# Inputs laid out by the host as the products read them, and keys projected turned, in a one-core decoder step

## The chip, the core and the metric

The kernel runs on one core of a Trainium2 chip. The core has TensorE (matrix products and transposes, results in PSUM), VectorE, ScalarE and POOL (GpSimd) for elementwise work, SP (SyncE) as the queue that issues most DMAs, and 16 DMA engines. The engines run their instructions in the order in which they were written down and wait for each other by semaphores. The metric is the device time of one execution in microseconds (us). Arrays that the Python function `kernel()` rearranges before the launch, and results that it rearranges after it, lie outside that time.

## The reference

One step of a decoder layer with 1024 features, for a prompt of 2048 tokens and for 8 sampled sequences of 8 new tokens, all in float32. The parts that matter here:

```python
z = jnp.einsum('bsd,dc->bsc', x, w_in)            # queries, keys, values, gates, mLSTM q/k/v
conv = conv_b + xpad[:, 0:S] * conv_w[0]          # + 3 more taps; then silu: mLSTM q and k
fox_h = _fox_prompt(fq, fk, fv, flogf)            # causal attention, 8 heads of 64, forget terms
(C, n, m), m_h = _mlstm_prompt(mq, mk, mv, ig, lf)
k_past = cache_k[l][page_table].reshape(DB, past, FOX_HEADS, FOX_HEAD_DIM)   # 8 x 8192 keys
sfox_h = _fox_sample(sq, sk, sv, slogf, k_past, v_past, logf_past)
mix = jnp.concatenate([fox_h, mn], axis=-1) @ w_o
x1 = _layer_norm(DN_ALPHA * x + mix, ln1_g, ln1_b)
hid = jnp.square(jax.nn.relu(x1 @ w1))
y = _layer_norm(DN_ALPHA * x1 + hid @ w2, ln2_g, ln2_b)
```

Besides y, new keys and values, log forget values, the mLSTM states and the last three columns of the convolution's input are returned.

## The kernel before

Each large product is made of three (`mm3`, L154 to L156): both operands are split into a high part (`split_hi`, ScalarE, L146) and a rest (`split_lo`, VectorE, L149), and high by high, high by rest and rest by high are summed in PSUM.

The work comes in stages.

*Projections (0 to 962 us).* `block_a` runs over four blocks of 512 tokens; block 0 also has the 64 sampled tokens as tile 16. `x_load` (L281) brings a tile of 128 tokens by 1024 features into one of two buffers named xn. `x_turn` transposes it on TensorE (L296, eight transposes for each tile), because a product contracts over partitions, and splits the result out of PSUM into xh and xl. `wload` (L249) brings 512 rows by 256 columns of w_in and splits them into whi and wlo. Products come in two forms. In `natural`, tokens are the stationary operand and the result has tokens on partitions (values, gates, keys). In the turned form, weights are stationary and the result has features on partitions (mLSTM q and k, queries). All products of this stage, and the transposes px, take PSUM from the same four buffers. `conv_setup` brings the convolution's weights and states and transposes them; at the end of blocks 0 and 3 the new convolution states are transposed back (cs_n L523 to L525, ch_n L531 to L533) for their outputs. Beside the projections run the mLSTM (`m_block`, `m_sample`) and the cached attention.

*Causal attention (to 1415 us), `phase_b`.* Keys are read back from the output k_prompt in groups of 512 tokens by 64 features (dup, L915), doubled by a POOL copy (L916), turned by four TensorE transposes (L936) and split into ks. Queries (L947) were stored turned and are read twice by two DMAs. Then come scores (L974, L975), exponentials (ScalarE, L1000), transposes of the weights (L1013) and products with values (L1022).

*Output projection (to 1656 us), `phase_o`*, with pieces of w_o (`half_wo`), and *feed-forward (to the end), `phase_c`*, in four blocks of tokens with pieces of w1 and w2 (wr, L1121).

*Cached attention, `sample_attention`.* A generator of 294 steps that runs beside the other stages: after so many microseconds of other products by the code's own estimates (`tick`, 5.6 in the projections, 5 from the output projection on) one more step is written down. Cached keys come by indirect DMAs on POOL's queue (`k_gather`, L1521) into a ring of pieces kT; two steps later VectorE transposes them in squares of 32 by 32 (`k_turn`, L1527); two steps after that `qk_step` (L1550) multiplies them with the queries, four heads side by side in the array. Values are gathered by `v_gather` (L1638) and multiplied by `pv_step` (sO, L1662). The keys of the new tokens are transposed on TensorE (L1472) out of a tile sqk.

The order of the instructions on each engine is set at compile time by the framework, which simulates a timeline (`schedule_with_timeline_sim=True`); a few orders are forced by hand (`first` for the first eight loads, `issue_after` for the steps of the generators). An instruction that comes too early on an engine holds up what is behind it.

Of the kernel before, what the change touches and what calls it, by code (L numbers as in the profile page):

```python
# [10 lines left out]
F32 = mybir.dt.float32  # L11
# [41 lines left out]
def body(ctx, tc, I, O, stages):  # L53
# [36 lines left out]
    sqk = []  # L90
# [92 lines left out]
    w_in = I["w_in"][0]  # L183
# [12 lines left out]
    def conv_setup():  # L196
        cwn = pa.tile([5, 1024], F32, name="cwn", tag="xn", bufs=2)
        SY.dma_start(cwn[0:4], I["conv_w"][0])
        SY.dma_start(cwn[4:5], I["conv_b"])
        pcw = ppa.tile([128, 8, 5], F32, name="px", tag="pm", bufs=4)  # L200
# [3 lines left out]
        scn = pa.tile([24, 1024], F32, name="scn", tag="xn", bufs=2)  # L204
        SY.dma_start(scn, I["state_conv"][0].rearrange("b j c -> (b j) c"))
        pcs = ppa.tile([128, 8, 24], F32, name="px", tag="pm", bufs=4)
        for j in range(8):
            T.transpose(pcs[:, j], scn[:, j * 128:(j + 1) * 128], ident[:24, :24])
        V.tensor_copy(scT.rearrange("p j b k -> p j (b k)"), pcs)
# [31 lines left out]
    def wload(cols):  # L241
# [17 lines left out]
    k_out = lambda t: (O["k_sample"].rearrange("l b t h d -> (l b t) (h d)") if t == 16  # L259
                       else O["k_prompt"].rearrange("l b s h d -> (l b s) (h d)")[t * 128:(t + 1) * 128])  # L260
# [17 lines left out]
    def x_load(*tiles):  # L278
        for t in tiles:
            xns[t] = pa.tile([128, D], F32, name="xn", bufs=2)  # L280
            first(SY.dma_start(xns[t][:tok_n(t)], x_of(t)))  # L281

    def x_turn(bi, t):
# [7 lines left out]
        xn = xns.pop(t)  # L291
        (xh, xl), s = xcol(bi, t)
        for hf in range(2):
            px = ppa.tile([128, 4, 128], F32, name="px", tag="pm", bufs=4)
            for k in range(4):
                T.transpose(px[:, k, :n], xn[:n, (hf * 4 + k) * 128:(hf * 4 + k + 1) * 128], ident[:n, :n])  # L296
# [132 lines left out]
    def block_a(bi):  # L429
# [3 lines left out]
        def natural(sink, *cols, hook=None, after=None):  # L433
            wh, wl = W0.pop() if W0 else wload(cols)
# [42 lines left out]
        for j in range(8):  # L477
            if j % 2 == 0:
                wh, wl = wload([(C_QK + j * 128, 256)])
# [37 lines left out]
        if pre:  # L517

            cs_n = pa.tile([24, 1024], F32, name="cs_n", tag="xn", bufs=2)
            for hf in range(2):  # L520
                pc = ppa.tile([24, 512], F32, name="px", tag="pm", bufs=4)
                for j in range(4):
                    T.transpose(pc[:, j * 128:(j + 1) * 128], scT[:, hf * 4 + j].rearrange("p b k -> p (b k)"), ident)  # L523
                A.copy(cs_n[:, hf * 512:(hf + 1) * 512], pc)
            SY.dma_start(O["conv_sample"].rearrange("l b j c -> (l b j) c"), cs_n)  # L525
        if bi == 3:
            ch_n = pa.tile([3, 1024], F32, name="ch_n", tag="xn", bufs=2)
            for hf in range(2):
                pc = ppa.tile([3, 512], F32, name="px", tag="pm", bufs=4)
                for j in range(4):  # L530
                    T.transpose(pc[:, j * 128:(j + 1) * 128], hist[:, hf * 4 + j], ident)  # L531
# [1249 lines left out]
```

## Time and profile before

| what | value |
|---|---|
| three runs | 3441.78, 3434.79, 3453.91 us; median 3441.78 |
| profiled execution, span from first to last instruction | 3435.1 us |
| TensorE busy | 3305.7 us (96%) |
| VectorE, ScalarE, POOL busy | 2174.9, 1365.7, 886.5 us |
| DMA | 646.37 MB, mean 188 GB/s |

The profile gives no other time for the profiled execution than its span. "PE" is TensorE's products and transposes, "PEld" its weight loads, "DVE" VectorE, "ACT" ScalarE. A row for a group names its line, engine and operation, the tiles written and read ("out<-in"), its shape and count, then its busy time and the mean of one instruction, then the idle time of its engine ahead of it and what ended that. A row of waits reads: who waited for whom, us in total, times, longest. TensorE's instructions overlap, so the mean duration of one is longer than the distance from one start to the next, and it is this distance that a product costs. "PEclk" is the clock granted to TensorE as a share of full speed.

### The profile page before, as it was taken

Reading aid. Unit: us, or ns where it says so; the run is one execution under the profiler, and the core shown is the slowest. Engines: PE = TensorE matmul, PEld = TensorE weight load, DVE = VectorE, ACT = ScalarE, POOL = GpSimd, SP = SyncE. Lnnn points to the kernel's source line nnn. Section 1 sums busy time; section 2 is a strip of 40 time slices with the busy share of each in tenths; the row PEclk is TensorE's granted clock in tenths of the full one; section 3 lists DMA queues with packets and bytes.
Section 4 is the critical chain, followed back from the end, with each engine's and each line's share of the span. In section 5 each row is a group of like instructions: output and inputs, shape, how many; then the busy total and the mean of one; then the engine's idle time right before and its main releaser. Section 6 shows DMA issues by size and latency. Waiting matters only on the chain.

```text
span 3435.1 us, 59551 instructions
## 1 busy us (share of the span) xinstructions
PE 3305.7 (96%) x22428; PEld 2682.1 (78%) x22428; DVE 2174.9 (63%) x5286; ACT 1365.7 (40%) x2818; POOL 886.5 (26%) x957
## 2 busy tenths in 40 slices
PE   9999998999989999999999999999999999999998
PEld 8998988888866666677777777777777777888887
DVE  5857757557468887655666667656666545645545
ACT  3333333233358888512323233332333333433332
POOL 0021221322322222276333324323234210100000
PEclk9999999999989999999999999999999999999999
DMA  6565765866653232487877768757669554432221
GB/s 177 141 193 161 238 203 164 271 221 205 224 173 92 74 80 60 154 290 250 292 254 230 260 195 314 267 192 272 230 217 313 197 183 145 164 122 85 82 80 65
DMA packets 428119, 646.37 MB, mean 188 GB/s; under 512 B 84092, under 2 KB 320960, under 8 KB 426936
## 3 DMA queue, kind: packets, MB, share of 16 engines
q1 hardware_dynamic: 351144, 363.35, 35.2%
q0 software_dynamic: 74304, 270.57, 21.5%
q10 hardware_dynamic: 2384, 8.65, 0.7%
q8 instruction: 177, 2.90, 0.3%
q14 instruction: 110, 0.90, 0.1%
HBM read 589.63 MB, written 52.83 MB: 187 GB/s over the span
## 4 chain that ended last, share of the span: by engine, by line
PE 75%; DMA 9%; DVE 6%; issue 5%; ACT 2%; POOL 2%; another core or an unknown queue 0%; SPq 0%; POOLq 0%; ACTq 0%; DVEq 0%
PE py L154 7%; PE py L156 7%; PE py L155 7%; PE ph L156 6%; PE ph L155 6%; PE ph L154 6%; PE po L1022 4%; PE pt L1013 4%; PE pm L154 4%; PE pm L156 4%; PE pm L155 4%; PE sO L1662 3%; PE sQ L1550 3%; DMA kT<-cache_k,idxK 2%; PE pS L974 2%
## 5 line engine op out<-in xcount | busy, mean ns | idle before, releaser
L1345 DVE TENSOR_TENSOR y<-y,py 128x512 f32<-128x512 f32 (+1 forms) x476 | 321.0, 681 | 335.1 <-PE py L156 307.3
L154 PE MATMUL ph<-x1h,wh 128*128 128x512 f32 (+1 forms) x1280 | 455.2, 356 | 3.8 <-ACT wh L146 1.8
L156 PE MATMUL ph<-x1h,wl 128*128 128x512 f32 (+1 forms) x1280 | 452.4, 355 | 3.3 <-DVE wl L149 2.4
L155 PE MATMUL ph<-x1l,wh 128*128 128x512 f32 (+1 forms) x1280 | 453.9, 355 | 1.1 <-DVE x1l L149 0.9
L154 PE MATMUL py<-wh,hh 128*128 128x512 f32 (+1 forms) x1088 | 436.1, 403 | 10.2 <-DVE y L1345 6.9
L1521 POOL DMA_INDIRECT kT<-cache_k,idxK x256 | 263.1, 1028 | 702.2 <-PE sQ L1550 641.6
L146 ACT ACTIVATE wh<-wr 128x1024 fp32r<-128x1024 f32 x268 | 277.5, 1055 | 416.0 <-PE py L156 189.8
L1527 DVE STREAM_TRANSPOSE kT<-kT 128x512 f32<-128x512 f32 x512 | 330.0, 685 | 177.5 <-DMA kT<-cache_k,idxK 161.2
L156 PE MATMUL py<-wh,hl 128*128 128x512 f32 (+1 forms) x1088 | 430.5, 396 | 0.0
L155 PE MATMUL py<-wl,hh 128*128 128x512 f32 (+1 forms) x1088 | 430.5, 396 | 0.0
L149 DVE TENSOR_TENSOR wl<-wr,wh 128x1024 fp32r<-128x1024 f32 x268 | 336.2, 1259 | 70.0 <-ACT wh L146 21.0
L154 PE MATMUL pm<-whi,xh 128*128 128x256 f32 (+2 forms) x1088 | 321.6, 296 | 13.5 <-ACT ch_n L532 4.1
L155 PE MATMUL pm<-wlo,xh 128*128 128x256 f32 (+2 forms) x1088 | 315.6, 290 | 1.2 <-DVE wlo L149 0.8
L156 PE MATMUL pm<-whi,xl 128*128 128x256 f32 (+3 forms) x1088 | 315.0, 290 | 1.2 <-issue 1.2
L154 PEld LDWEIGHTS ph<-x1h,wh 128*128 128x128 f32 x1280 | 241.2, 188 | 45.0 <-issue 6.5
L156 PEld LDWEIGHTS ph<-x1h,wl 128*128 128x128 f32 x1280 | 241.4, 189 | 39.5 <-DVE wl L149 4.6
L155 PEld LDWEIGHTS ph<-x1l,wh 128*128 128x128 f32 x1280 | 241.2, 188 | 37.8 <-issue 2.9
L154 PEld LDWEIGHTS py<-wh,hh 128*128 128x128 f32 (+1 forms) x1088 | 201.2, 185 | 73.0 <-issue 14.1
L156 PEld LDWEIGHTS py<-wh,hl 128*128 128x128 f32 (+1 forms) x1088 | 201.3, 185 | 53.2 <-issue 2.5
L155 PEld LDWEIGHTS py<-wl,hh 128*128 128x128 f32 (+1 forms) x1088 | 201.7, 185 | 44.1 <-issue 2.5
L154 PE MATMUL pm<-xh,whi 128*128 128x256 f32 (+1 forms) x768 | 225.7, 294 | 6.0 <-ACT qi L495 6.0
L1638 POOL DMA_INDIRECT vt<-cache_v,idxV x158 | 165.2, 1046 | 242.7 <-PE sO L1662 162.8
(369 smaller groups left out, 6892.4 us busy)
## 6 DMA issues: line engine op xcount, KB each, us to landing
wr<-w SPq DMA_DIRECT2D x256, 512.0 KB
wra<-w_in SPq DMA_DIRECT2D x112, 512.0 KB
Rb<-dR SPq DMA_DIRECT2D x128, 128.0 KB
xn<-x_prompt SPq DMA_DIRECT2D x16, 512.0 KB
qn<-dq SPq DMA_DIRECT2D x128, 64.0 KB
wr<-w_o SPq DMA_DIRECT2D x16, 512.0 KB
xr<-dmix SPq DMA_DIRECT2D x16, 512.0 KB
y<-x_prompt SPq DMA_DIRECT2D x16, 512.0 KB
```

The costliest lines, as they stand in the source:

```text
L146: last["ACT"] = A.activation(dst, src, AF.Copy, scale=scale)
L149: r = (eng or V).tensor_tensor(dst, src, hi.bitcast(F32), op=OP.subtract)
L154: T.matmul(ps, wh, xh, start=first, stop=False)
L155: T.matmul(ps, wh, xl, start=False, stop=False)
L156: last["PE"] = T.matmul(ps, wl, xh, start=False, stop=stop)
L1013: T.transpose(pt[:, k], sc[i][0][k0 // 4][:, k * 128:(k + 1) * 128], ident)
L1022: last["PE"] = T.matmul(po[c:c + 64, q0:], z["vn"][:, k], PT[:, k - k0, q0:], start=(k < 2), stop=(k >= nk - 2), skip_group_check=True)
L1345: V.tensor_tensor(y, y, ps, op=OP.add)
L1521: G.indirect_dma_start(out=piece(n), out_offset=None, in_=ck, in_offset=IO(ap=idxK[:, b, j // 2, j % 2:j % 2 + 1], axis=0))
L1527: V.transpose(x, x)
L1550: r = T.matmul(pq[h4 * 32:h4 * 32 + 32, hg].rearrange("p (k f c) -> p k f c", k=2, f=4), z["qb"][:, hd], kv, start=(db == 0), stop=(db == ...
L1638: G.indirect_dma_start(out=vt.rearrange("p f c -> p (f c)"), out_offset=None, in_=cv, in_offset=IO(ap=idxV[:, b, (kt % 4) * 4 + kt // 4, f ...
```

## The change

`kernel()` lays out, before the launch, x (each tile turned, features on partitions), the cached keys (per page, in two halves of four heads each, 32 features by 1024 values of head, feature half and token), the convolution's weights and states, the mLSTM normaliser, and all pieces of w_in, w1 and, for the output projection of the prompt, w_o as contiguous [128, n] arrays. It also turns six results back after the launch. On the chip the transposes for these go (px, pcw, pcs, cs_n, ch_n, nn, pn_), and `k_turn` with its VectorE transposes. Keys are projected in the turned form by the loop of the queries, stored as k_prompt [512, 2048], and read back by two DMAs for each group of 512 tokens, as queries are; the POOL copy and the transposes L936 go, and so does the tile sqk with its transposes.

```diff
-        cwn = pa.tile([5, 1024], F32, name="cwn", tag="xn", bufs=2)
...
-        for j in range(8):
-            T.transpose(pcw[:, j], cwn[:, j * 128:(j + 1) * 128], ident[:5, :5])
-        V.tensor_scalar(cw, pcw, 0.5, None, op0=OP.mult)
...
+        SY.dma_start(cw, I["conv_wb"])
+        V.tensor_scalar(cw, cw, 0.5, None, op0=OP.mult)
+        SY.dma_start(scT, I["state_conv"])
...
-    def wload(cols):
+    def wload(*cols):
...
-            wr = pa.tile([128, 4 * 272], F32, name="wra", bufs=2)[:, :4 * n].rearrange("p (k c) -> p k c", k=4)
-            o = 0
-            for c0, m in cols:
-                first(SY.dma_start(wr[:, :, o:o + m], w_in[kg * 512:(kg + 1) * 512, c0:c0 + m].rearrange("(k p) c -> p k c", p=128)))
-                o += m
+            wr = pa.tile([128, 4 * 272], F32, name="wra", bufs=2)[:, :4 * n]
+            first(SY.dma_start(wr, dap(I["w_in"], w_at[cols] + kg * 512 * n, [[4 * n, 128], [1, 4 * n]])))
+            wr = wr.rearrange("p (k c) -> p k c", k=4)
...
-            first(SY.dma_start(xns[t][:tok_n(t)], x_of(t)))
+            n = 8 * tok_n(t)
+            first(SY.dma_start(xns[t][:, :n], I["xs_t"] if t == 16 else I["xp_t"][t]))
...
-        xn = xns.pop(t)
+        xn = xns.pop(t)[:, :8 * n].rearrange("p (k c) -> p k c", k=8)
         (xh, xl), s = xcol(bi, t)
-        for hf in range(2):
-            px = ppa.tile([128, 4, 128], F32, name="px", tag="pm", bufs=4)
-            for k in range(4):
-                T.transpose(px[:, k, :n], xn[:n, (hf * 4 + k) * 128:(hf * 4 + k + 1) * 128], ident[:n, :n])
-            dh = xh[:, hf * 4:hf * 4 + 4, s]
-            split_hi(dh, px[:, :, :n])
-            split_lo(xl[:, hf * 4:hf * 4 + 4, s], px[:, :, :n], dh)
+        split_hi(xh[:, :, s], xn)
+        split_lo(xl[:, :, s], xn, xh[:, :, s])
...
-            cs_n = pa.tile([24, 1024], F32, name="cs_n", tag="xn", bufs=2)
-            for hf in range(2):
-                pc = ppa.tile([24, 512], F32, name="px", tag="pm", bufs=4)
-                for j in range(4):
-                    T.transpose(pc[:, j * 128:(j + 1) * 128], scT[:, hf * 4 + j].rearrange("p b k -> p (b k)"), ident)
-                A.copy(cs_n[:, hf * 512:(hf + 1) * 512], pc)
-            SY.dma_start(O["conv_sample"].rearrange("l b j c -> (l b j) c"), cs_n)
+            SY.dma_start(O["conv_sample"], scT)
...
-            ch_n = pa.tile([3, 1024], F32, name="ch_n", tag="xn", bufs=2)
...
-            SY.dma_start(O["conv_prompt"].rearrange("l b j c -> (l b j) c"), ch_n)
+            SY.dma_start(O["conv_prompt"], hist)
...
-        for j in range(4):
+        for j in range(8):
+            c, jj = divmod(j, 4)
             if j % 2 == 0:
-                wh, wl = wload([(j * 128, 256)])
+                wh, wl = wload((j * 128, 256))
                 if pre:
                     qr = ps_.tile([32, 8, 8, 8], F32, name="qr", tag="vt", bufs=2)
             cs = slice((j % 2) * 128, (j % 2) * 128 + 128)
+            scale = 1.0 if c else 0.125
...
+                    if c:
+                        st = pa.tile([128, 256], F32, name="st", bufs=4)[:, :64]
+                        A.copy(st, ps[:, 0:64])
+                        SY.dma_start(O["k_sample"][jj * 128:(jj + 1) * 128], st)
...
-                A.activation(st, ps[:, w - 256:], AF.Copy, scale=0.125)
-                SY.dma_start(dq[j, :, t0 + i * 256:t0 + i * 256 + 256], st)
+                A.activation(st, ps[:, w - 256:], AF.Copy, scale=scale)
+                a = t0 + i * 256
+                SY.dma_start(O["k_prompt"][jj * 128:(jj + 1) * 128, a:a + 256] if c else dq[jj, :, a:a + 256], st)
...
-            natural(sink, (512 + i * 256, 256))
...
+                SY.dma_start(dqb[c, :, :, jj // 2 * 64:jj // 2 * 64 + 64].rearrange("b p c -> p b c"), qr.rearrange("p b i t -> p b (i t)"))
...
-        def twice(src, t):
-
-            n = pb.tile([128, t, 2, 64], F32, name="dup", tag=f"dup{t}", bufs=3)
-            SY.dma_start(n[:, :, 0], src.rearrange("(i t) c -> t i c", t=128))
-            G.tensor_copy(n[:, :, 1], n[:, :, 0])
-            return n
...
+            kn = pb.tile([128, 512], F32, name="kn", bufs=3)
+            for d in range(2):
+                SY.dma_start(kn[d * 64:d * 64 + 64], kp[h * 64:h * 64 + 64, g * 512:(g + 1) * 512])
+            return kn
...
-            pt = ppb.tile([128, 4, 128], F32, name="pt", bufs=3)
-            for i in range(4):
-                T.transpose(pt[:, i], kn[:, i].rearrange("p d c -> p (d c)"), ident)
-            pf = pt.rearrange("p i c -> p (i c)")
             k = z["ks"][:, g * 512:(g + 1) * 512]
-            split_hi(k, pf)
-            split_lo(k[64:128], pf[64:128], k[64:128])
+            split_hi(k, kn)
+            split_lo(k[64:128], kn[64:128], k[64:128])
...
-        SY.dma_start(r, I["w_o"][0, q * 256:(q + 1) * 256, hf * 512:(hf + 1) * 512].rearrange("(k p) c -> p k c", p=128))
+        SY.dma_start(r, I["w_o2"][hf, q].rearrange("p (k c) -> p k c", k=2))
...
-        return [piece(I["w1"][0][kg * 512:kg * 512 + 512, fc * 256:fc * 256 + 256].rearrange("(k p) c -> p k c", p=128)) for kg in range(2)]
+        return [piece(I["w1"][fc, kg].rearrange("p (k c) -> p k c", k=4)) for kg in range(2)]
...
+    fk = ps_.tile([128, 2], F32, name="fk")
+    for f in range(2):
+        V.tensor_scalar(fk[:, f:f + 1], fo[:, 0:1], 32.0 * f, None, op0=OP.add)
...
-    ck = I["cache_k"][0].rearrange("g (t f) h d -> (g t) (f h d)", f=2)
+    ck = I["cache_k"].rearrange("g f d c -> (g f d) c")
...
-        p = pps.tile([32, 8, 64], F32, name="sT", tag="sX", bufs=1)
-        for i in range(8):
-            T.transpose(p[:, i], sqk[0][:, (g * 8 + i) * 32:(g * 8 + i) * 32 + 32], ident[:64, :64])
-        qr = ps_.tile([32, 8, 8, 8], F32, name="qr", tag="vt", bufs=2)
-        A.copy(qr.rearrange("p b i t -> p i b t"), p.rearrange("p i (b t) -> p i b t", t=8))
-        SY.dma_start(dqb[1, :, :, g * 64:g * 64 + 64].rearrange("b p c -> p b c"), qr.rearrange("p b i t -> p b (i t)"))
...
-    def k_turn(n):
-
-        for i in range(2):
-            x = piece(n)[:, i * 512:(i + 1) * 512]
-            V.transpose(x, x)
...
-                    kv = bass.AP(tensor=a0.tensor, offset=a0.offset + hd * 32,
-                                 ap=[list(a0.ap[0]), [d * 2048, 2], [512, 4], [1, 32]])
-                    r = T.matmul(pq[h4 * 32:h4 * 32 + 32, hg].rearrange("p (k f c) -> p k f c", k=2, f=4), z["qb"][:, hd], kv,
+                    kv = bass.AP(tensor=a0.tensor, offset=a0.offset + hg * 1024 + (h4 * 2 + db) * 128,
+                                 ap=[list(a0.ap[0]), [d * 2048, 2], [1, 128]])
+                    r = T.matmul(pq[h4 * 32:h4 * 32 + 32, hg].rearrange("p (k c) -> p k c", k=2), z["qb"][:, hd], kv,
...
-        if 0 <= g < GA and r >= 2:
-            k_turn(4 * g + 2 * r - 4)
-            k_turn(4 * g + 2 * r - 3)
-        if NA + 2 < n < 258:
-            if n == NA + 3:
-                k_turn(NA)
-            k_turn(n - 2)
...
+    a["xp_t"] = a["x_prompt"].reshape(16, 128, 8, 128).transpose(0, 3, 2, 1).reshape(16, 128, 1024)
+    a["xs_t"] = a["x_sample"].reshape(NS, 8, 128).transpose(2, 1, 0).reshape(128, 8 * NS)
+    ck = a["cache_k"][0]
+    a["cache_k"] = ck.reshape(ck.shape[0], 32, 4, 2, 4, 2, 32).transpose(0, 3, 6, 4, 5, 2, 1).reshape(ck.shape[0], 2, 32, 1024)
+    a["w_in"] = np.concatenate([pieces(a["w_in"][0], c) for c in W_PASSES])
...
+    a["w1"] = a["w1"][0].reshape(2, 4, 128, 16, 256).transpose(3, 0, 2, 1, 4).reshape(16, 2, 128, 1024)
...
+    r["k_prompt"] = r["k_prompt"].T.reshape(1, 1, S, FH, 64)
```

More of the change, by code (lines that the diff above doesn't have):

```diff
@@ L719, in m_block @@
         SY.dma_start(O["C_prompt"][0, 0].rearrange("h d e -> d h e"), Cs[:, :, 0:128])
[L720 to L724 removed]
+        nn = pm.tile([128, 4], F32, name="nn", tag="sm", bufs=1)
+        V.tensor_copy(nn, Cs[:, :, 128])
+        SY.dma_start(O["n_prompt"], nn)
         yield 1
@@ L844, in m_sample @@
             V.tensor_tensor(n1[:, :, h], n1[:, :, h], pn2, op=OP.add)
[L845 to L850 removed]
+        SY.dma_start(O["n_sample"], n1)
         norm_out(hh, 64, og, S)
@@ L1779 @@
     r = run_bass_kernel_spmd(nc, [arrays], core_ids=[0])
-    return tuple(r.results[0][k] for k, _ in OUTS)
+    return laid_out({k: np.asarray(r.results[0][k]) for k, _ in OUTS})
```

106 lines of the change are left out of this document (39 added, 67 removed).

## The prediction

> **What bounds the kernel now.** I read the head of the page first, then the busy times cut into the kernel's stages, then TensorE's own waits, then the granted clock around those waits.
>
> ```profile
> span 3435.1 us, 59551 instructions
> PE 3305.7 (96%) x22428; PEld 2682.1 (78%) x22428; DVE 2174.9 (63%) x5286; ACT 1365.7 (40%) x2818; POOL 886.5 (26%) x957
> ```
>
> The stages are projections (0 to 962), causal attention (to 1415), output projection (to 1656), feed-forward with cached attention beside it (to 2740) and without (to the end):
>
> ```profile
> core 0: us, PE busy (x) PEld busy (x) DVE busy (x) ACT busy (x) POOL busy (x), PEclk, DMA share, GB/s
> 0.00:962.00 962.00, 903.35 (x7682) 848.22 (x7682) 619.77 (x1727) 331.08 (x720) 221.58 (x261) 0.98 0.64 199
> 962.00:1415.00 453.00, 438.20 (x3002) 303.10 (x3004) 348.84 (x1375) 366.17 (x1024) 121.41 (x204) 0.98 0.32 89
> 1415.00:1656.00 241.00, 226.24 (x1394) 168.31 (x1390) 141.69 (x315) 61.09 (x89) 143.46 (x113) 0.98 0.77 266
> 1656.00:2740.00 1084.00, 1061.23 (x6561) 794.70 (x6562) 694.91 (x1356) 364.40 (x600) 353.37 (x342) 0.99 0.72 249
> ```
>
> TensorE is the bound in every stage; the second-busiest engine is ScalarE in the causal attention (366 of 453) and VectorE elsewhere. So a TensorE instruction that goes is worth its whole spacing, and VectorE time is worth only the TensorE waits that it causes. All TensorE idleness is 3435.1 - 3305.7 = 129 us, 59 of it in the first stage. The waits that matter:
>
> ```profile
> PE px L296 <- DVE xl L149: 6.4, 1, 6.4
> PE sO L1662 <- DMA vt<-cache_v,idxV: 5.4, 3, 2.4
> PE px L296 <- DMA xn<-x_sample: 4.8, 1, 4.8
> PE px L296 <- DMA xn<-x_prompt: 4.7, 3, 2.2
> PE pm L154 <- ACT ch_n L532: 4.1, 1, 4.1
> PE pm L154 <- DVE xl L149: 4.0, 1, 4.0
> PE pm L154 <- ACT cs_n L524: 3.4, 1, 3.4
> ```
>
> A wait costs more than itself. Two stretches of idleness and what follows each (columns as above):
>
> ```profile
> 101.60:103.90 2.30, 0.01 (x1) 0.00 (x0) 2.10 (x5) 2.30 (x8) 0.00 (x0) 1.00 0.86 257
> 103.90:110.70 6.80, 5.67 (x27) 5.59 (x28) 6.80 (x25) 2.07 (x7) 2.43 (x4) 0.50 0.48 146
> 469.30:472.50 3.20, 1.01 (x10) 0.98 (x10) 2.94 (x7) 1.36 (x4) 0.00 (x0) 1.00 0.86 233
> 472.50:475.90 3.40, 3.40 (x19) 3.40 (x18) 3.05 (x8) 1.32 (x4) 0.00 (x0) 0.51 0.61 156
> ```
>
> And for the whole run:
>
> ```profile
> core 0: 3435.1 us, clock 0.984
> ```
>
> After a wait of some 2 us or more the granted clock is 0.5 for 3.4 or 6.8 us, which loses another 1.7 or 3.4 us. Over the span the mean clock is 0.984, so (1 - 0.984) x 3435 = 55 us are lost in this way.
>
> The Trainium skill, "TensorE: Matmul & The Clock Gate", Part 1, has the clock halve only after at least one idle window of about 3.4 us. The trace differs: the second pair above shows half clock behind a wait of 2.2 us. By the page that wait would be free of the 1.7 us and the forecast one or two us later; I go by the trace.
>
> **The change part by part.** Spacings, start to start, from the timeline of TensorE:
>
> ```profile
> 161.15 0.31 PE L156 MATMUL pm<-xh,wlo 128*128 128x320 f32 x1
> 161.29 0.30 PE L154 MATMUL pm<-xh,whi 128*128 128x320 f32 x1
> ...
> 170.46 0.28 PE L156 MATMUL pm<-whi,xl 128*64 128x256 f32 x1
> 170.57 0.28 PE L154 MATMUL pm<-whi,xh 128*64 128x256 f32 x1
> ...
> 176.38 0.29 PE L156 MATMUL pm<-whi,xl 128*128 128x256 f32 x1
> 176.50 0.28 PE L154 MATMUL pm<-whi,xh 128*128 128x256 f32 x1
> ...
> 240.62 2.04 PE L296 MATMUL px<-ident,xn 128*128 128x128 f32 x16
> 251.12 1.04 PE L296 MATMUL px<-ident,xn 128*128 128x128 f32 x8
> ...
> 1123.79 1.04 PE L1013 MATMUL pt<-ident,S 128*128 128x128 f32 x8
> 1124.58 0.37 PE L974 MATMUL pS<-ks,qh 128*128 128x256 f32 x1
> 1127.06 0.60 PE L936 MATMUL pt<-ident,dup 128*128 128x128 f32 x4
> 1127.59 0.44 PE L1022 MATMUL po<-PT,vn 128*64 128x256 f32 x2
> ```
>
> *x is laid out turned.* Seventeen tiles lose 8 transposes each (L296). Eight cost 2.04 - 1.04 = 1.0 us. The first two tiles' lie in the start's wait, so 15 x 1.0 = 15 us go. ScalarE and VectorE now split 1024 columns at once from SBUF.
>
> *Keys of the prompt, turned and read twice by DMA.* 32 groups of 4 transposes (L936) go. One group takes 0.53 us by its row, or 4 x 0.79/8 = 0.40 us by the like transposes L1013: 13 to 17 us, taken 14. The POOL copy goes too. One more DMA is issued on SP for each group (64 in place of 32). ScalarE now waits for the load itself, ahead of the exponentials queued behind it. The nearest row is the query's load, split in the same way (what the engines waited for at that tile: us, times):
>
> ```profile
>   DMA qn<-dq: 2.8, 2
> ```
>
> That is 2.8 us for 64 queries; for 32 groups half of that, 1.4 us on ScalarE, and nothing on TensorE as long as ScalarE has the 87 us to spare that the second stage shows.
>
> *Keys projected turned.* In blocks 1 to 3 it is the same 192 matmuls of 256 columns at 0.12 us. In block 0 the sampled tile's 48 products at 0.11 us go (5.3 us) and 96 products widen from 256 to 320 columns, 0.12 to 0.145 us (2.4 us): 3 us gained. VectorE gets 16 small copies of new keys in block 0, like those of the queries:
>
> ```profile
> L562 DVE TENSOR_SCALAR qr<-pm x16: 205/217/225, 143.0 to 165.5; 32x64 f32<-32x64 f32 x16
> ```
>
> That is 16 x 0.217 = 3.5 us; SP gets two more stores. VectorE's lost work below covers the copies; without it a product would wait for its buffer, 3.5 us at most.
>
> *Small turns.* Convolution weights and states (16 in, 16 out), new keys (16), normalisers (3): 51 transposes at 0.1 us, 5 us. The four stores of tiny rows that come instead are waited for by nobody on TensorE; SP has them in its queue as before.
>
> *Waits that hung on these.* With cs_n gone its 3.4 us and 3.4 us of half clock lose their cause; ScalarE stood behind mLSTM work there, so some will return: I take 5 of 6.8. ch_n likewise: 3 of 4.1 + 1.7. At the starts of blocks 1 to 3 the waits on xl and x_prompt come to 15 us (6.4 + 4.7 + 4.0), with half clock of 3.4 to 6.8 us behind each 22. Products of a block's first tiles no longer queue behind transposes of its later ones. Against that, x's buffer is now freed by VectorE's split, not by the transposes, some 2 us later, and so is the load of the tile two further on. Between 0 and 22 gained I take 8; if the load becomes the wait, 10 lost.
>
> *Cached keys laid out turned.* 512 VectorE transposes go:
>
> ```profile
> L1527 DVE STREAM_TRANSPOSE kT<-kT 128x512 f32<-128x512 f32 x512 | 330.0, 685 | 177.5 <-DMA kT<-cache_k,idxK 161.2 <-issue 15.8
> L1550 PE MATMUL sQ<-kT,qb 128*32 128x256 f32 x2048 | 129.9, 390 | 3.7 <-DVE kT L1527 3.2 <-issue 0.3
> L1662 PE MATMUL sO<-vt,PTs 128*32 128x256 f32 x1264 | 86.5, 388 | 5.4 <-DMA vt<-cache_v,idxV 5.4
> ```
>
> VectorE is freed of 330 us of work and 161 us of standing in front of a DMA, neither on the path except through small waits. sQ now waits for the gather directly, two steps after the turn did, so it has more time, not less. I price all TensorE gains from a freer VectorE, with the larger packets of the weight pieces, at 3 us in the first stage and 8 of the 38 us idle in the two stages from 1415 to 2740. sQ reads contiguous columns in place of runs of 32: contiguous sO takes 86.5/1264 = 68 ns, sQ now 129.9/2048 = 63. From these rows the ends are 10 us lost and 10 gained; taken at 0, its own row.
>
> *Weight pieces.* Same bytes in 4 KB rows in place of 1 or 2 KB, and no separate 8-column loads:
>
> ```profile
> q1 hardware_dynamic: 351144, 363.35, 35.2%
> q0 software_dynamic: 74304, 270.57, 21.5%
> ```
>
> A 1 KB packet of q1 takes 0.352 x 16 x 3435 / 351144 = 55 ns, a 3.6 KB one of q0 159 ns: 53 and 44 ns per KB. The loads get shorter; their worth is in the waits above.
>
> **Sum.** TensorE work 15 + 14 + 3 + 5 = 37; waits 5 + 3 + 8 + 3 + 8 = 27; together 64. The profiled span of 3435 becomes 3371; the page gives no other time of that execution, and the median of the runs is 3441.8, 6.7 more. So 3441.8 - 64 = 3378.
>
> **Rivals.**
> *All the idleness goes too.* For it: VectorE loses a fifth of its time. The four stages shown stand idle 111 us, 106 without the wait for the first load; half of it and half of the clock's 55 us on top of 37 give 3441.8 - 37 - 53 - 27 = 3325. Against: the waits on VectorE shown come to 14 us (6.4 + 4.0 + 3.2), the rest hang on others.
>
> *The transposes were cover.* ScalarE at 366 of 453 us keeps the pace of the causal attention and the split of x that of the block starts. Then 14, 15 and 8 fall away, and 27 remain: 3415. Against: TensorE stands idle only 15 of the 453 us there, so little keeps it back now.
>
> *Slower: value gathers late in the first stage.* The products sO alone in that stage, and one gather on the chain that ended last (start, us, what):
>
> ```profile
> 581.00:962.00 381.00, 24.32 (x336) 10.07 (x332) 0.97 0.70 227
> ...
> 716.61 11.66 DMA vt<-cache_v,idxV
> ```
>
> With 16 products a step these are 21 steps, 18 us apart, and a value buffer is refilled only after the step before: two issues on POOL, then up to 11.7 us to land. Weight packets four times as long ahead of it delay it. From a landing of about 16 us each step waits. At 18 us that is 2.5 us of waiting and 1.7 us of half clock, 21 times, 88 us: 3466. For it: three of these waits are there already (5.4 us in the table of waits). Against: a whole 512 KB load is 128 x 159 ns / 16 = 1.3 us, and three or four would have to be in front. The Trainium skill, "DMA: Bandwidth & Descriptors", Queues, rings and completion order, speaks for this rival: each DMA engine takes the queues in turn, one packet of descriptors each. By that rule a gather's turns come later when the weights' packets grow.
>
> **How the numbers follow.** The forecast 0.63, within 3355 to 3400; all idleness 0.13; cover 0.14, of which a third ends within 0.5%; slower 0.10, a tenth of it within 0.5%. About 0.5%, 17 us, is what a measurement can tell from no change. Faster: 0.63 + 0.13 + 0.09 = 0.85; same 0.05 + 0.01 = 0.06; slower 0.09. The range of 3340 to 3425 leaves out the slower rival and the far half of the first.
>
> **What will show it.** TensorE busy near 3269, with px L296 and pt L936 gone; VectorE 330 us lower; no wait on cs_n and ch_n, and clock near 0.99. Wrong if new waits for xl or x at the block starts exceed 22 us, if ScalarE waits for keys' loads cost TensorE in the causal attention, if sO waits for vt grow past 5.4 us, or if sQ's mean rises.

## The result and the profile after

The changed kernel takes 3393.73 us (median of four runs, 3391.37 to 3398.82), the kernel before on the same chip 3442.91 us: a ratio of 0.9855, 95% interval 0.9839 to 0.987. That is 49 us saved where 64 were forecast. The profiled execution of after spans 3390.5 us, 44.6 less than that of before; the rest of the 49 is the difference of one execution to another.

The head of the page after, its clock, and two queues (packets, time as a share of 16 engines):

```profile
span 3390.5 us, 58224 instructions
PE 3263.4 (96%) x22065; PEld 2642.0 (78%) x22065; DVE 1884.5 (56%) x4774; ACT 1361.9 (40%) x2795; POOL 870.8 (26%) x925
```

```profile
core 0: 3390.5 us, clock 0.985
```

```profile
q1 hardware_dynamic: 239032, 367.55, 35.4%
q0 software_dynamic: 74304, 270.57, 22.1%
```

The first queue moves 1% more bytes than before in a third fewer packets, and its share of the time is the same (35.4% against 35.2%).

TensorE is busy 3305.7 - 3263.4 = 42.3 us less. Part of that is half clock. These are the sums over all stretches in which the granted clock was 0.5, for before and then for after (us of such stretches, then the busy time of each engine in them):

```profile
sum 109.00, PE 81.32 PEld 65.39 DVE 71.52 ACT 29.04 POOL 29.80; mean PE 4.07 PEld 3.27 DVE 3.58 ACT 1.45 POOL 1.49
```

```profile
sum 100.24, PE 58.45 PEld 46.64 DVE 39.89 ACT 24.52 POOL 24.46; mean PE 4.17 PEld 3.33 DVE 2.85 ACT 1.75 POOL 1.75
```

At half clock at most half of TensorE's busy time is lost: 41 us before and 29 after, some 11 less. (Taking 1 minus the clock times the span, 55.0 and 50.9 us, counts half clock in which TensorE stands idle as well.) The remaining 31 us are work that went, known to some 7 us, for other executions of after are busy 3257.2 and 3256.1 us where this one is busy 3263.4. All idleness falls from 129.4 to 3390.5 - 3263.4 = 127.1 us: by 2 us, though VectorE lost 290 us of work. So the saving is work and half clock; the waits gave back what they lost.

The busy times by stage, each cut at the first instruction of the next stage, before and then after:

```profile
core 0: us, PE busy (x) PEld busy (x) DVE busy (x) ACT busy (x) POOL busy (x), PEclk, DMA share, GB/s
0.00:966.30 966.30, 904.61 (x7690) 849.06 (x7690) 620.89 (x1729) 332.57 (x723) 222.34 (x263) 0.97 0.65 199
966.30:1418.80 452.50, 438.37 (x3005) 302.94 (x3005) 349.16 (x1376) 367.18 (x1025) 123.22 (x204) 0.98 0.31 88
1418.80:1656.10 237.30, 224.84 (x1381) 167.65 (x1381) 140.35 (x313) 58.59 (x85) 140.99 (x111) 0.98 0.78 269
1656.10:3435.10 1779.00, 1737.94 (x10354) 1362.48 (x10354) 1064.54 (x1870) 607.32 (x986) 399.91 (x381) 0.99 0.58 197
```

```profile
0.00:926.80 926.80, 871.63 (x7451) 818.89 (x7451) 535.38 (x1576) 328.69 (x700) 237.42 (x268) 0.98 0.67 208
926.80:1371.90 445.10, 422.40 (x2881) 293.32 (x2881) 347.91 (x1377) 364.37 (x1026) 107.66 (x167) 0.98 0.35 97
1371.90:1607.50 235.60, 225.23 (x1381) 167.66 (x1381) 104.49 (x246) 58.62 (x85) 141.66 (x111) 0.98 0.80 270
1607.50:3390.50 1783.00, 1744.11 (x10354) 1362.10 (x10354) 896.74 (x1577) 610.28 (x986) 384.08 (x381) 0.99 0.58 197
```

Nearly all of the saving lies in the projections, 7 us in the causal attention, and the feed-forward stage with the cached attention beside it is 4 us longer, although VectorE is rid of 360 of the 512 transposes from 1372 us on.

TensorE's waits after (us in total, times, longest):

```profile
PE pt L960 <- ACT S L947: 13.1, 4, 11.4
PE sO L1598 <- DMA vt<-cache_v,idxV: 12.7, 4, 7.1
PE pm L153 <- ACT whi L145: 8.5, 1, 8.5
PE sT L1535 <- ACT PTs L1557: 7.7, 1, 7.7
PE pS L921 <- ACT qh L145: 7.5, 2, 7.3
```

The waits that the forecast tied to the parts that went are gone: the 6.4, 4.7 and 4.0 at the block starts, 4.1 on ch_n, 3.4 on cs_n, 22.6 us together. In their place stand: at the start of the causal attention 7.3 + 11.4 where before had 4.0 + 2.8 + 1.9 there, 10 us more; values' gathers 12.7 where before had 5.4, 7 more; and a wait of 7.7 on PTs at L1535, 4.6 more than the 3.1 that the like wait of L1619 had. Together some 22 us. (The 8.5 at the start stands where x_sample's 4.8 and the first tiles' transposes stood; the first product begins at 8.5 us in both.)

The longest of them is seen in two timelines of after, POOL's and ScalarE's (start, us, what, in brackets the idle time before it and what ended that):

```profile
919.33 1.04 POOL L1463 DMA_INDIRECT kT<-cache_k,idxK  x1 [0.18 <-PE mm L585]
...
925.65 0.94 POOL L1463 DMA_INDIRECT kT<-cache_k,idxK  x1 [0.30 <-issue]
929.39 1.28 POOL L914 TENSOR_TENSOR nd<-nl,dmask 128x128 f32<-128x128 f32 x3 [2.79 <-DMA nl<-dnl]
```

```profile
926.41 0.42 ACT L145 ACTIVATE qh<-qn 128x256 fp32r<-128x256 f32 x1 [5.60 <-DMA qn<-dq]
936.89 0.63 ACT L145 ACTIVATE ks<-kn 128x512 fp32r<-128x512 f32 x1 [10.07 <-DMA kn<-k_prompt]
938.95 0.40 ACT L947 ACTIVATE S<-S,mx 128x128 f32<-128x128 f32 x1 [1.42 <-DVE mx L935]
```

Six gathers of 512 KB go out on POOL at 919 to 926 us, ahead of the first masks nd; the first query lands at 926.4, and the second group of keys keeps ScalarE standing for 10.07 us, with the first exponentials behind it. Before, the gathers went out behind the copy of the keys and the first masks, which wait for their own load:

```profile
962.37 0.40 POOL L916 COPY dup<-dup 128x256 f32<-128x256 f32 x1
966.99 1.28 POOL L967 TENSOR_TENSOR nd<-nl,dmask 128x128 f32<-128x128 f32 x3 [4.22 <-DMA nl<-dnl]
968.44 1.06 POOL L1521 DMA_INDIRECT kT<-cache_k,idxK  x1 [0.17 <-issue]
```

The cached keys' product keeps its cost:

```profile
L1486 PE MATMUL sQ<-kT,qb 128*32 128x256 f32 x2048 | 127.7, 382 | 7.1 <-DVE rl L1545 3.3 <-issue 1.6 <-DMA kT<-cache_k,idxK 1.4
```

### The profile page after: what moved, and what is told of

It reads as the page before. It is cut to its first block, busy times and chain, and to the rows that moved or that the text cites. A ratio compares the mean times of both kernels' runs of the same rounds, so it can differ in the third digit from the quotient of the medians.

```text
span 3390.5 us, 58224 instructions
## 1 busy us (share of the span) xinstructions
PE 3263.4 (96%) x22065; PEld 2642.0 (78%) x22065; DVE 1884.5 (56%) x4774; ACT 1361.9 (40%) x2795; POOL 870.8 (26%) x925
## 3 DMA queue, kind: packets, MB, share of 16 engines
q1 hardware_dynamic: 239032, 367.55, 35.4%
## 4 chain that ended last, share of the span: by engine, by line
PE 48%; DMA 3%; DVE 2%; issue 1%; ACT 1%; POOL 1%; another core or an unknown queue 0%; SPq 0%; POOLq 0%; ACTq 0%; DVEq 0%
PE py L153 7%; PE py L155 7%; PE py L154 7%; PE ph L153 7%; PE ph L155 7%; PE ph L154 7%; PE sO L1598 3%; PE sQ L1486 2%; DMA wr<-w 2%; PE sT L1555 1%; DVE wl L148 1%; PE pw L154 0%; PE pw L155 0%; PE pw L153 0%
## 5 line engine op out<-in xcount | busy, mean ns | idle before, releaser
L153 PE MATMUL pm<-xh,whi 128*128 128x256 f32 (+1 forms) x1024 | 301.9, 295 | 0.7 <-issue 0.4
L154 PE MATMUL pm<-xl,whi 128*128 128x256 f32 (+1 forms) x1024 | 297.9, 291 | 2.4 <-issue 2.3
L155 PE MATMUL pm<-xh,wlo 128*128 128x256 f32 (+1 forms) x1024 | 296.9, 290 | 2.8 <-issue 2.7
L153 PE MATMUL pm<-whi,xh 128*128 128x256 f32 (+2 forms) x816 | 238.6, 293 | 9.9 <-ACT whi L145 8.5
L154 PE MATMUL pm<-wlo,xh 128*128 128x256 f32 (+2 forms) x816 | 233.9, 287 | 0.6 <-DVE wlo L148 0.6
```

The costliest lines, as they stand in the source:

```text
L153: T.matmul(ps, wh, xh, start=first, stop=False)
L154: T.matmul(ps, wh, xl, start=False, stop=False)
L155: last["PE"] = T.matmul(ps, wl, xh, start=False, stop=stop)
```

## The experiments

The first four ran on a second chip (before 3426.43 us there), the other eight on a third (before 3419.27 and 3425.65 us). Times are set against each other on one chip alone; ratios are to before on that chip, with 95% intervals. The theory at the start: the forecast's work term holds; the waits came back because of the handover's gathers and of the cached keys' layout.

**The handover's gathers.** `beside` already holds a step's instructions behind the last one of TensorE, VectorE and ScalarE; this adds POOL.

```diff
-                G.tensor_tensor(nd, nl[:, qt * 128:n], dmask, op=OP.add)
+                last["POOL"] = G.tensor_tensor(nd, nl[:, qt * 128:n], dmask, op=OP.add)
```

> The kernel after, with one entry more: the six cached-key gathers issued at the start of the causal attention may not be put ahead of POOL's masks nd. Theory: in the changed kernel these gathers (3 MB) go out at 919 to 927 us, in the same stretch as the loads of the first queries and keys, because the copies of keys that stood ahead of them on POOL are gone; they make qh wait 7.3 us and the first exponentials 11.4 us. With the gathers behind the masks the idleness at the handover falls from 21.4 us (2.8 + 7.3 + 11.4) to 9 or less, the half clock behind it from 24 us to 10, and the time from 3394 to between 3375 and 3384. Rival: the first loads of keys and queries are late by themselves (short rows, many issues on SP); then the waits stay above 15 us together and the time between 3388 and 3397.

3378.75 us, 0.9849 (0.9825 to 0.9873). The waits at the handover are 4.1 and 4.8 us, but by the ratio it is no better than after on the first chip. So it was run again beside after itself.

> The kernel after, unchanged, beside the next three on one chip. On the chip of the first four runs the kernel before took 3426 us and not 3443, so the times there can't be set against after's 3394. Expected by after's ratio of 0.9855: 3377 where before takes 3426, 3393 where it takes 3443, and at the handover two waits of 7 and 11 us. If the handover's waits belong to one chip or one execution, the second is far shorter here.

After here: 3385.14 us, 0.9909 (0.9894 to 0.9924), with 7.1 and 11.5 us at the handover. The same program saves 34 us on this chip and 49 on the first; the handover's waits are the same.

> The gathers behind POOL's masks once more, now beside after on the same chip. On the other chip the handover's waits were 4.1 and 4.8 us and the ratio to before 0.9849, no better than after's 0.9855. Theory (the gathers make the handover's waits): 8 to 15 us less than after. Rival (they cost nothing on most executions, or what is gained comes back as later waits of sO and sQ in the stages behind): within 5 us of after.

3381.04 us, 0.9896 (0.9879 to 0.9914): 4 us less than after, within both intervals. Where it went shows when both are cut at the same instruction, the end of POOL's last product hh ahead of the causal attention: 914.3 us in after, 922.9 with the gathers held. The rows are the 30 us of the handover, the 100 us behind it and the rest of the causal attention, first after, then with the gathers held:

```profile
914.30:944.30 30.00, 10.26 (x40) 6.11 (x42) 9.75 (x45) 8.35 (x23) 9.99 (x16) 0.60 0.90 260
944.30:1044.30 100.00, 97.44 (x658) 67.65 (x659) 85.14 (x327) 86.96 (x247) 23.87 (x37) 1.00 0.42 127
1044.30:1367.20 322.90, 315.15 (x2190) 219.83 (x2188) 252.78 (x1009) 270.19 (x760) 79.32 (x120) 1.00 0.27 76
```

```profile
922.86:952.86 30.00, 19.28 (x100) 12.54 (x100) 17.61 (x76) 17.31 (x48) 6.62 (x14) 0.77 0.77 204
952.86:1052.86 100.00, 93.34 (x628) 63.48 (x629) 83.41 (x317) 83.16 (x234) 28.84 (x43) 1.00 0.50 148
1052.86:1369.70 316.84, 311.21 (x2160) 216.63 (x2158) 248.59 (x988) 266.87 (x748) 78.23 (x120) 1.00 0.27 75
```

In the handover TensorE is busy 9 us more and the clock is 0.77 in place of 0.60: the gathers do make a good part of the handover's waits (4.0 and 4.6 us are left). In the next 100 us, where the held gathers now stand between the masks, 4 us are lost again. From the cut to the output projection it is 446.8 us against 452.9, 6 less; but the cut itself comes 8.6 us later, although the edit touches nothing ahead of it. The theory's mechanism holds; its price of 8 to 15 us doesn't show in the time.

**x turned on the chip again.**

```diff
-            first(SY.dma_start(xns[t][:, :n], I["xs_t"] if t == 16 else I["xp_t"][t]))
+            first(SY.dma_start(xns[t][:tok_n(t)], x_of(t)))
...
-        split_hi(xh[:, :, s], xn)
-        split_lo(xl[:, :, s], xn, xh[:, :, s])
+                T.transpose(px[:, k, :n], xn[:n, (hf * 4 + k) * 128:(hf * 4 + k + 1) * 128], ident[:n, :n])
...
+            split_hi(dh, px[:, :, :n])
+            split_lo(xl[:, hf * 4:hf * 4 + 4, s], px[:, :, :n], dh)
```

> The kernel after, with x loaded in rows of tokens and turned on TensorE again; all else as after. Theory (transposes cost their own time, the waits at block starts belong to them): 15 us of transposes come back, and of the waits at the three block starts some 5 to 10 us: 3409 to 3419, TensorE busy 15 to 18 us higher. Rival 1 (the transposes were cover for the weights' split, and the time goes into other waits): 3391 to 3400. Rival 2 (the 22 us of waits all belong to them): 3425 or more.

3408.16 us, 0.9953 (0.9932 to 0.9974): some 30 us more than the two neighbours on its chip that have x laid out (3378.75 and 3378.1). After itself wasn't run there; by its three ratios on other chips (0.9855, 0.9909, 0.9886) it would take 3377 to 3395 us, and the price is 13 to 31. TensorE is busy 11 to 16 us more than in the neighbours, and waits at the block starts are back, all for x's loads:

```profile
PE px L283 <- DMA xn<-x_prompt: 12.8, 3, 5.9
```

Three waits, one for each block start, none of them in after. With the products they make 24 to 29 us, before any half clock, where the theory had 15 to 25. So waits at the block starts come with x's turns, and more of them than the theory's 5 to 10 us; that it is nearly all 22, as rival 2 has it, isn't shown, for the base is known only to the width above.

**The weights of the projections as before.**

```diff
-            first(SY.dma_start(wr, dap(I["w_in"], w_at[cols] + kg * 512 * n, [[4 * n, 128], [1, 4 * n]])))
+            for c0, m in cols:
+                first(SY.dma_start(wr[:, :, o:o + m], w_in[kg * 512:(kg + 1) * 512, c0:c0 + m].rearrange("(k p) c -> p k c", p=128)))
+                o += m
```

> The kernel after, with the weights of the projections (w_in) loaded from their own layout again, in rows of 1 KB and with the two loads of 8 columns. Theory (the size of the packets is worth nothing here): 3389 to 3398, and sO's waits for value gathers stay near 12.7 us. Rival 1 (packets four times as long hold up the gathers): the waits of sO on vt fall to some 5 us and the time to 3383 to 3388. Rival 2 (long rows shorten the weights' loads and so the waits on whi): 3399 or more.

3378.1 us, 0.9849 (0.9826 to 0.9873), below the ranges of all three, which were worked out from the first chip's 3394. On its chip it can be set only against its neighbour with long rows and held gathers (3378.75); its profiled span, 3378.7 us, is 1 to 3 us below those of after on the third chip (3382.0 and 3379.6). The wait for values' gathers with rows of 1 KB, then in that neighbour with rows of 4 KB:

```profile
PE sO L1598 <- DMA vt<-cache_v,idxV: 21.1, 10, 5.3
```

```profile
PE sO L1598 <- DMA vt<-cache_v,idxV: 19.2, 8, 6.6
```

Rows four times as long don't lengthen the waits. By "DMA: Bandwidth & Descriptors" (the Trainium skill, section Queues, rings and completion order) the queues are taken in turn packet by packet; a price of that on the gathers isn't seen in these two. Nor does a gain of long rows show, though the two differ in the held gathers as well.

**Keys as before** (projected in rows of tokens, copied, turned; the diff is the change's own, backwards).

```diff
-            kn = pb.tile([128, 512], F32, name="kn", bufs=3)
-            for d in range(2):
-                SY.dma_start(kn[d * 64:d * 64 + 64], kp[h * 64:h * 64 + 64, g * 512:(g + 1) * 512])
-            return kn
+            return twice(kp[g * 512:(g + 1) * 512, h * 64:h * 64 + 64], 4)
```

> The kernel after, with the keys projected in rows of tokens, copied twice by POOL and turned on TensorE, and the new keys turned, as before; all else as after. The transposes (14 us), the block 0 products (3) and the small turns (2) come back, 19 us. Theory of the handover (POOL's copies stand again ahead of the gathers): the waits at the start of the causal attention fall back from 21.4 us to about 9, with 6 us of half clock less, so only 0 to 8 us are left of the 19: 3393 to 3402. Rival (the handover's waits are not POOL's order): 3408 to 3416.

3396.32 us, 0.9909 (0.9887 to 0.9932): inside the theory's range, but 18 us above the neighbours, as the work alone has it (1 to 20 us above after by its three ratios); TensorE is busy 17 to 22 us more than in these. The causal attention is 456.0 us long, against 445.0 and 444.8. On POOL the first masks stand ahead of the gathers again. The handover's waits are 2.8 + 2.8 + 6.3 + 1.9 + 2.1 = 16 us there, less than after's 21, but not the theory's 9. The values' waits are longer than the neighbours' (28.2 us against 19.2 and 21.1); that this is what took the gain back isn't shown.

**The cached keys alone, both ways.** Before with the laid out keys, and after without them (its diff is this one backwards):

```diff
-    ck = I["cache_k"][0].rearrange("g (t f) h d -> (g t) (f h d)", f=2)
+    ck = I["cache_k"].rearrange("g f d c -> (g f d) c")
...
-            k_turn(4 * g + 2 * r - 4)
-            k_turn(4 * g + 2 * r - 3)
...
-            k_turn(n - 2)
...
-                                 ap=[list(a0.ap[0]), [d * 2048, 2], [512, 4], [1, 32]])
+                                 ap=[list(a0.ap[0]), [d * 2048, 2], [1, 128]])
```

> The kernel before, with nothing changed but the cached keys: laid out turned by the host, so that VectorE's 512 transposes go and the products read the gathered block in runs of 128. Theory A (VectorE's 330 us are off the path): within 5 us of before, 0.9985 to 1.0015. Theory B (a freer VectorE takes waits away): 10 to 25 us faster, 0.993 to 0.997. Theory C (by the undone parts, which sum to 31 us for x and 20 for keys against 49 for the whole): it costs time, 5 to 15 us slower, 1.0015 to 1.0045, with longer waits of sO for value gathers.

> The kernel after, with the cached keys in their own layout and turned by VectorE again (512 instructions, 330 us). Theory A: within 5 us of after. Theory B: 10 to 25 us slower than after. Theory C: 5 to 15 us faster than after, and the waits of sO for value gathers back from 12.7 us towards 5.4.

Alone: 3425.36 us, 1.0018 (1.0006 to 1.0029), slower than before. Taken back out of after: 3370.85 us, 0.9855 (0.9841 to 0.987), 14 us faster than after on the same chip, the intervals apart. Both as theory C has it: 330 us less of VectorE make the kernel 6 to 14 us slower. Of its other half, sO's waits back towards 5.4 us, a part is seen: 17.2 in place of 26.3 us. The granted clock goes with the time: 0.987 in all four executions with the transposes, 0.982 to 0.985 in the five of after beside them. The products' group in after on this chip, then with VectorE turning the keys:

```profile
L1486 PE MATMUL sQ<-kT,qb 128*32 128x256 f32 x2048 | 128.8, 386 | 6.6 <-DMA kT<-cache_k,idxK 5.8 <-ACT PTs L1557 0.6
```

```profile
L1466 DVE STREAM_TRANSPOSE kT<-kT 128x512 f32<-128x512 f32 x512 | 331.1, 686 | 224.2 <-DMA kT<-cache_k,idxK 223.6
L1489 PE MATMUL sQ<-kT,qb 128*32 128x256 f32 x2048 | 127.9, 386 | 3.8 <-ACT PTs L1560 1.9 <-issue 1.0 <-DVE kT L1466 0.9
```

With the transposes it is VectorE that stands in front of late gathers, 223.6 us that cost sQ 0.9; without them TensorE stands there itself. The clock adds to it. Two such waits in after on this chip, each with what follows it (columns as in the windows above):

```profile
2461.00:2464.90 3.90, 1.07 (x18) 0.42 (x17) 0.69 (x1) 0.00 (x0) 1.88 (x2) 1.00 1.03 413
2466.10:2469.60 3.50, 3.50 (x9) 2.71 (x9) 3.02 (x11) 1.99 (x2) 2.42 (x2) 0.51 1.03 404
2018.00:2021.00 3.00, 0.59 (x12) 0.16 (x8) 0.69 (x1) 0.25 (x1) 2.00 (x2) 1.00 1.03 421
2021.00:2025.00 4.00, 4.00 (x30) 2.87 (x23) 2.16 (x9) 1.07 (x1) 1.94 (x3) 1.00 1.02 407
```

The DMA engines are full in all four rows, which fits gathers that are late for want of bandwidth; the first wait, 2.8 us, is followed by 3.5 us at half clock, the second, 2.4 us, by none. From the first transpose of the feed-forward stage to the end (some 20 us more than the cut above) after takes 1798.8 us, with VectorE's transposes 1780.3. Of the 18.5 us, TensorE's idleness makes 4 and half clock some 6 (38.6 us of it, 22.4 of them busy, against 21.2 and 9.9). The other 8 are busy time of the same 10480 products and transposes, and their cause isn't found. In the projections it is the other way round: 922.1 us after, 934.1 with the transposes. The order of the instructions speaks for the planner's part in it: of the 32 pairs of steps on TensorE's queue the thirtieth stands behind 15,291 other products and transposes in after and behind 15,390 with VectorE's transposes. Slower gathers from the new layout would be a rival: from that stage on they take a median of 8.3 us from issue to landing in after and 8.4 with the old layout, but the longest 17.3 against 12.7. So the reading is that the planner, freed of VectorE's time, puts products earlier, and that there the gather is late.

**Where the stages part, and whether a hop is enough.** The base once more:

> The kernel after, unchanged, as the base of the next three. Its ratio to before was 0.9855 on the first chip and 0.9909 on the second: between these here.

3386.88 us, 0.9886 (0.9866 to 0.9906).

```diff
-        G.indirect_dma_start(out=piece(n), out_offset=None, in_=ck, in_offset=IO(ap=idxK[:, b, j // 2, j % 2:j % 2 + 1], axis=0))
+        G.indirect_dma_start(out=piece(n), out_offset=None, in_=ck if n < NA else cn, in_offset=IO(ap=idxK[:, b, j // 2, j % 2:j % 2 + 1], axis=0))
...
+        if NA + 2 < n < 258:
+            if n == NA + 3:
+                k_turn(NA)
+            k_turn(n - 2)
```

> The kernel after, with both layouts of the cached keys in memory: the 76 pieces of the first stage are gathered turned, the other 180 in their own layout and turned by VectorE (360 instructions) as before. Theory (the laid out keys gain some 12 us in the first stage, where VectorE is short, and lose some 18 in the feed-forward stage, where TensorE waits for gathers which the planner had taken to be there, and the clock is halved behind each wait): 12 to 20 us faster than after; the first stage is as long as after's, the feed-forward stage 10 us or more shorter. Rival (the two differences of the stages belong to each other, for the background's steps only move from one stage to the other): within 5 us of after.

3387.58 us, 0.9883 (0.9862 to 0.9905): as after. The feed-forward stage gains what the theory said, 1790.8 us against 1800.9, and sQ's waits on gathers fall from 6.3 to 0.5 us; the thirtieth pair stands behind 15,390 again. But the projections, whose work is after's but for 16 small index instructions, take 933.6 us against 919.9. Part of that is a wait that after doesn't have, TensorE's and behind it ScalarE's (140 to 160 us):

```profile
PE mn L672 <- ACT hh L602: 4.7, 1, 4.7
```

```profile
ACT Wm L632 <- DMA Wm<-dM: 10.9, 1, 10.9
```

ScalarE stands 10.9 us in front of a load of the mLSTM, with work that TensorE needs queued behind it: another order of the same instructions. The other part can be the order or one execution against another: the kernel with the gathers held reaches the causal attention at 913.0 us on the second chip and at 927.6 on the third, after itself on the third at 922.1 and 919.9. So 14 us in the projections come without any change of the work there, and the 12 us that the laid out keys seemed to gain are no larger. What a freer VectorE is worth in that stage stays open.

```diff
+    def k_turn(n):
+
+        x = piece(n)[:, 0:1]
+        V.tensor_copy(x, x)
```

> The kernel after, with one copy of a single column onto itself by VectorE in the place of each former pair of transposes: the product then waits for VectorE, which has waited for the gather, and VectorE has no work of note. Theory (it is the transposes' time in the plan that had put the products later on TensorE's queue; a hop without time changes nothing): within 4 us of after, the waits of TensorE only named otherwise. Rival (a product must not stand directly behind a gather; the hop over VectorE takes the wait): 10 us or more faster than after.

3405.65 us, 0.9935 (0.9915 to 0.9954): 19 us slower than after, against both. The feed-forward stage is 1803.9 us long, no shorter than after's, with the products in the planner's order as early as after's (the thirtieth pair behind 15,288); so the hop doesn't take the wait, it only renames it (sQ waits 12.2 us on VectorE). The projections are 946.1 us long, 26 more than after's, the largest difference seen; whether it is the order again isn't shown.

> The last but one together with the gathers held behind POOL's masks at the handover. Theory: the masks' 4 us (3381 against 3385 on the second chip) come on top: 3 to 8 us faster than with the layouts alone, 0.974 to 0.981 of before. Rival (the handover's gain is given back in the stage behind it, as half of it was before): the same as with the layouts alone within 2 us.

3374.92 us, 0.9841 (0.982 to 0.9862): 12 us faster than after, the intervals just apart, and 13 below the same without the masks. Its profiled execution spans 3385.4 us, above its median, and shows the handover's waits at 4.4 and 4.4 us. Cut at hh as above, it is 448.5 us to the output projection, against 453.9 without the masks: 5 us. The clock is 0.985 to 0.989 in its executions and 0.983 to 0.986 in those without the masks; where the rest of the 13 comes from isn't shown. With the version without laid out cached keys (0.9855, 14 us faster than after on that chip) it is one of two whose intervals lie below those of both kernels on their chip.

## Why the prediction was right and where it failed

The sign and the range held: 3393.7 lies within 3340 to 3425, and beyond the 0.5% that a measurement tells. The likeliest case's own range, 3355 to 3400, holds it too. Of its mechanism the work held and the waits held only in part. The sum was 15 us too good, and that it was no further off is partly luck: waits that went altogether and new ones that the sum doesn't have cancel in it. One program's saving also differs by as much from chip to chip (49, 34 and 39 us).

Two of the four signs of being wrong that the prediction names came: ScalarE's wait for keys cost TensorE time in the causal attention, and sO's waits for vt grew past 5.4 us, to 12.7. The other two didn't: no waits of that kind at the block starts, and sQ's mean fell from 390 to 382 ns.

*The term of work, 37 us:* 31 measured, to some 7 us. By parts, x's transposes 15 (11 to 16 more busy time with x turned on the chip), keys 14 + 3 + 2 (17 to 22 with keys as before). The price by spacing, start to start, fits both.

*The term of waits, 27 us:* 2 of idleness and some 11 of half clock measured. The 55 us of clock that the prediction starts from were too many: TensorE was busy in 81 of the 109 us at half clock, so at most 41 were lost. The steps:
- cs_n, ch_n and the block starts: their waits went entirely, 22.6 us before any clock, where 16 with the clock were taken. The block starts were mis-sized: 8 taken, some 13 and the clock behind them seen when x was turned again. The wait of 7.7 that came stands there with x turned again too (6.8), and neither with keys (1.2) nor with cached keys (1.1) as before: it is not x's later buffer.
- "I price all TensorE gains from a freer VectorE ... at 3 us in the first stage and 8": this step failed, in sign. The cached keys' layout costs 6 us put into before and 14 in after. "sQ now waits for the gather directly, two steps after the turn did, so it has more time, not less" overlooked that the planner doesn't keep the steps' places: late in the stage the products stand 99 places earlier with VectorE's transposes gone. That waits and half clock in the feed-forward stage follow from it is shown by turning the keys on VectorE there alone (10 us back); the whole of the 14 us isn't accounted for.
- "nothing on TensorE as long as ScalarE has the 87 us to spare that the second stage shows": failed at the stage's start, where there is no earlier work to spend. One wait of 10.07 us for keys cost TensorE one of 11.4.
- "The POOL copy goes too" was costed at nothing. It stood, with the first masks and their 4.2 us of waiting, ahead of six gathers on POOL's queue; with it gone the planner put the gathers first, and they met the first loads of the stage. Holding them behind the masks takes 6 us off the handover and its stage.

*The rival of the transposes as cover* finds no support for x and keys: against the neighbours both came back with their own time and, for x, with waits. *The rival of late value gathers* had a true core: the waits grew from 5.4 to 12.7 us, on the third chip they are 26.3. But it took the weights' packets for the cause, and rows of 1 KB give the same waits as rows of 4 KB; and there are 4 to 11 such waits in the traces, not one at each of 21 steps. *The rival that all idleness goes* is out.

*The weight pieces* were priced in the waits, together with VectorE; alone they are worth nothing that shows. *sQ's row* was right: 129.9 before, 127.7 after.

Open: what the planner's order makes of the projections. Three programs with the same work for TensorE there take 919.9, 933.6 and 946.1 us, each in one profiled execution.

## What to carry to other kernels

An instruction that goes is worth its spacing on the bounding engine, and that part of a forecast held best here. Work off the path is another matter: an engine off the path can stand in front of a late transfer at no cost, where the bounding engine would stand there itself, and an instruction ahead of a transfer on an in-order queue sets when that transfer starts; ask of both what moves up when they go. Where a planner sets the order, each edit can order the whole program anew, and a difference in a stage (here 14 us without any change of its work) must be checked against an edit that changes nothing there.

## What was not expected of the hardware

One program saved 49 us on the first chip (0.9855) and 34 and 39 on the third (0.9909, 0.9886), with intervals that don't overlap between the first and the 0.9909. Between the two on the third chip the granted clock makes the difference up: over all executions it averages 0.9836 for after and 0.9855 for before in the first set, 0.9842 and 0.9843 in the second, and 0.0019 of 3390 us is 6 us. What differs on the first chip isn't shown. A wait of 2.8 us was followed by 3.5 us of half clock and one of 2.4 us by none, with the DMA engines full in both: and the forecast's pair has half clock behind 2.2 us, so the limit isn't sharp. The Trainium skill ("TensorE: Matmul & The Clock Gate", Part 1) gives an idle window of some 3.4 us; these waits are shorter.
